# The opening of a streamed encoder layer: TensorE's order held fixed, adaLN weights in other buffers, small loads later, one Newton round, and dt in two passes

## The chip, the cores and the metric

The kernel runs on one core of a Trainium2 chip. It computes in fp32. The metric is the device time of one execution in microseconds; lower is better. One execution of the program was also profiled, and its trace gives the start and length of every instruction on TensorE (PE), VectorE (DVE), ScalarE (ACT), GpSimd (POOL) and the DMA queues that SyncE (SP) and POOL issue.

## The reference

One inference step of a hybrid trunk of two layers, for a prompt of 256 tokens and a sample of 64 (320 together, model width 2048). Each layer modulates an RMS norm by a vector that comes from the condition `c` through a large weight (adaLN), mixes, and adds a gated norm of the result:

```python
def modulate(x, c, w_ada, b_ada, g_pre):
    mod = jax.nn.silu(c) @ w_ada + b_ada
    shift, scale, gate = jnp.split(mod[:, None, :], 3, axis=-1)
    return rms_norm(x, g_pre) * (1 + scale) + shift, gate
...
for layer in range(DEPTH):                      # DEPTH = 2
    hp, gate_p = modulate(xp, c_prompt, ...)    # 256 tokens
    hs, gate_s = modulate(xs, c_sample, ...)    # 64 tokens
    # even layer: one input projection for z, x/B/C, dt, q, k, v, gate;
    # SSD heads and sliding-window attention, one output projection
    # odd layer: u, gb, gc, g; short causal convolution; output projection
    xp = xp + gate_p * rms_norm(op, norm_post[layer])
```

In the even layer `dt = softplus(dt_raw + dt_bias)` has 32 columns, one for each SSD head. The outputs are both token streams and the new caches and states.

## The kernel before

**Products.** A token's features lie on partitions: activations are tiles of [128 features, 320 tokens], 16 k-tiles for the width of 2048. Every large product is made of fp32 numbers that are split into a rounded part and a remainder: weights in `wh` and `wl`, activations in `hh` and `hl`. A k-tile of a unit (128 output features) takes three matmuls with 320 columns: `wh x hh`, `wh x hl` and `wl x hh` (lines 168, 169, 170). `split` makes `wh` on ACT (L148) and from it `wl` on DVE (L149), for eight weight tiles [128, 8 x 128] at a time. `block` loads 16 tiles of weights into a pool of three buffers (`wp`, tag `w`), splits them, and appends a job; jobs are run two blocks later, and between quarters of a job `tick` lets other work in.

**Who sets the order.** The program text gives an order, and a scheduler then places each engine's instructions by its own estimate of when their operands are ready. So on PE, matmuls of one unit can stand among those of another, and an adaLN matmul or a transpose can be moved by some places.

**The opening.** The modulation of the first layer is not known when the program starts, so the first 24 units of the input projection (4 of K, 4 of V, then q and gate for two pairs of heads) go by pieces of K: `PIECES = ((0,1),(1,1),(2,2),(4,4),(8,4),(12,4))`, called stages 0 to 5 here (`j` in the code, and the first digit in the names `ws00` to `ws55`). In each stage all 24 units (`s_0` to `s_23`) take that piece, and `start_unit` adds their PSUM into fp32 tiles: with ACT in stage 0 (L404), with DVE behind it (L415, tiles `acc`, `q`, `g`). Between units stand the adaLN matmuls for the next piece: `ada_first` for tiles 0 and 1 (L362, PSUM `adaf`), and `ada_pe` for quarters of a block (L218, PSUM `adap`). `ada_end` copies the sums from PSUM with ACT (L262, `adar`), transposes them on PE (L264, `adat`) and adds the bias on DVE into `mod` (L268, L273, L275). Block 7 of the adaLN is summed on DVE instead (`ada_side`, L249, `adac`, from tiles `adas`). When the sums of a piece are there, `modulate` makes `mt` on DVE (L340), `hh` on ACT (L341) and `hl` on DVE (L342), in segments of 256 and 64 tokens. In stage 5 the V units are transposed on PE (L419, `vp`) before the attention starts. The first matmul behind the opening goes to a PSUM tile `pq`.

**The norm.** `sumsq` squares x with ACT (L324) and adds with DVE (L351) into two sums; these are merged, summed over partitions on PE (`ss0t`), and `rstd` finds the reciprocal root from the bits of the exponent and three Newton rounds (L302 to L307), spreads it over partitions on PE (`r0b`) and copies it to SBUF (`rsb`, L353).

**Small loads.** Thirteen loads for attention and SSD (cached K and V, sinks, convolution weights and states, dt's bias) are issued by POOL right behind `ada_first(0)`.

**dt.** The unit of dt is a unit like the others: 16 k-tiles x 3 matmuls (`pdt`, with `wdth` and `wdtl`), though only 32 of its 128 output rows are used. `steps` and `time_steps` then transpose it to tokens.

## Time and profile before

| | before |
|---|---|
| runs | 2179.76, 2177.35, 2173.21 us; median 2177.35 |
| profiled execution | span 2172.8 us (the three runs lie 0.4 to 7.0 above it) |
| PE busy | 2130.5 us (98%), 15582 matmuls |
| DVE busy | 1417.7 us (65%) |
| ACT busy | 887.1 us (41%) |
| POOL busy | 152.4 us (7%) |
| DMA | 408.81 MB, mean 188 GB/s |

Busy time is the sum of an engine's instructions with overlaps counted once. A wait row reads: engine, output tile and line of the instruction that waited, the engine, tile and line of what it waited for, and then the microseconds in total, the number of times, and the longest. In a timeline row the first number is the start in us from the beginning of the span and the second the length; `x4` at its end means four instructions of the same kind in a row.

### The profile page before, as it was taken

How to read it: one execution, taken by the hardware profiler on the slowest of the kernel's cores; microseconds unless marked ns; L12 is line 12 of the kernel's file. 1: busy time of each engine (PE TensorE's matmuls, PEld its weight loads, DVE VectorE, ACT ScalarE, POOL GpSimd, SP SyncE). 2: the span in 40 equal slices, each digit the busy share in tenths (PEclk: the TensorE clock that was granted, in tenths of full speed). 3: DMA queues.
4: the chain of work that ended last, by engine and by line, in shares of the span. 5: the costliest groups of instructions: out<-in, count | busy, mean ns of one | idle time of the engine just before them, and what ended most of it. 6: DMA issues, size and time to landing. Idle time of an engine off the chain costs nothing.

```text
span 2172.8 us, 38057 instructions
## 1 busy us (share of the span) xinstructions
PE 2130.5 (98%) x15582; PEld 2054.2 (95%) x15582; DVE 1417.7 (65%) x2351; ACT 887.1 (41%) x1446; POOL 152.4 (7%) x370
## 2 busy tenths in 40 slices
PE   7999999999999999999999999999999999999997
PEld 5899988899999999987999999999999999999996
DVE  5876888888577878996755555556345564444444
ACT  5233454543455565355433333333333333333343
POOL 1000000000123123102000000000000000000001
PEclk9999999999999999999999999999999999999998
DMA  8896545466455555776444444545444544444441
GB/s 314 327 325 209 182 156 180 165 225 226 162 197 175 180 177 195 273 257 244 174 161 176 174 167 169 179 157 198 155 166 164 175 171 144 155 153 141 154 155 68
DMA packets 85758, 408.81 MB, mean 188 GB/s; under 512 B 10544, under 2 KB 11472, under 8 KB 46416
## 3 DMA queue, kind: packets, MB, share of 16 engines
q1 hardware_dynamic: 80496, 392.22, 51.4%
q0 software_dynamic: 5088, 14.16, 2.2%
q8 instruction: 122, 2.00, 0.4%
q14 instruction: 52, 0.43, 0.1%
HBM read 400.35 MB, written 5.99 MB: 187 GB/s over the span
## 4 chain that ended last, share of the span: by engine, by line
PE 94%; DVE 2%; DMA 1%; ACT 1%; issue 1%; POOL 0%; SPq 0%; POOLq 0%; ACTq 0%; DVEq 0%
PE pc L168 13%; PE pc L170 13%; PE pc L169 13%; PE s L168 3%; PE s L170 3%; PE s L169 3%; PE px L168 2%; PE px L170 2%; PE px L169 2%; PE pq L168 2%; PE poe L168 2%; PE pod L168 2%; PE pod L170 2%; PE poe L169 2%; PE pq L170 2%; PE pq L169 2%
## 5 line engine op out<-in xcount | busy, mean ns | idle before, releaser
L249 DVE SCALAR_TENSOR_TENSOR adac<-adas,cs,adac 128x512 f32<-128x512 f32 x420 | 300.8, 744 | 56.1 <-DMA adas<-in_wada 56.1
L926 POOL COPY ncc<-cp 128x2 f32<-128x2 f32 x32 | 6.0, 187 | 932.9 <-DVE cp L924 932.9
L218 PE MATMUL adap<-adaw,cs 128*32 128x128 f32 x1152 | 42.2, 277 | 2.5 <-DMA adaw<-in_wada 2.5
L218 PEld LDWEIGHTS adap<-adaw,cs 128*32 128x32 f32 x1152 | 30.9, 110 | 10.8 <-issue 6.8
L500 ACT ACTIVATE pr<-s,mx 128x192 f32<-128x192 f32 (+2 forms) x80 | 30.0, 388 | 25.2 <-DVE mx L494 16.6
L644 POOL COPY nca<-xp 128x3 f32<-128x3 f32 x24 | 24.2, 1009 | 199.6 <-ACT xp L642 199.6
L931 DVE SCALAR_TENSOR_TENSOR cc<-cp,ccw,cc 128x322 f32<-128x322 f32 x64 | 35.3, 551 | 1.1
L924 DVE TENSOR_TENSOR cp<-pc,u 128x256 f32<-128x256 f32 x31 | 13.2, 425 | 30.6 <-PE pc L170 30.4
L341 ACT ACTIVATE hh<-mt,mod 128x256 fp32r<-128x256 f32 x64 | 23.7, 420 | 20.9 <-DVE mt L340 20.7
L678 ACT ACTIVATE sg<-sg,acum 128x128 f32<-128x128 f32 (+1 forms) x96 | 28.8, 373 | 6.3 <-POOL sg L670 6.3
L415 DVE TENSOR_TENSOR g<-s,g 128x320 f32<-128x320 f32 x40 | 19.0, 485 | 12.3 <-PE s L170 12.3
L649 DVE SCALAR_TENSOR_TENSOR cv<-xp,cw,cv 128x323 f32<-128x323 f32 x48 | 26.4, 551 | 0.3
L939 DVE TENSOR_TENSOR sgg<-pc,sgg 128x320 f32<-128x320 f32 x31 | 15.2, 489 | 17.3 <-PE pc L170 17.1
L849 DVE TENSOR_TENSOR oo<-poe,oo 128x320 f32<-128x320 f32 x16 | 7.9, 492 | 25.6 <-PE poe L170 25.6
L415 DVE TENSOR_TENSOR q<-s,q 128x320 f32<-128x320 f32 x40 | 18.9, 486 | 8.0 <-PE s L170 7.8
L362 PE MATMUL adaf<-w,cs 128*32 128x128 f32 x128 | 10.2, 308 | 13.6 <-ACT ss L324 13.1
L415 DVE TENSOR_TENSOR acc<-s,acc 128x320 f32<-128x320 f32 x32 | 15.3, 488 | 11.3 <-PE s L170 11.2
L342 DVE SCALAR_TENSOR_TENSOR hl<-mt,mod,hh 128x256 fp32r<-128x256 f32 x64 | 21.5, 379 | 1.4 <-ACT hh L341 1.4
L362 PEld LDWEIGHTS adaf<-w,cs 128*32 128x32 f32 x128 | 8.0, 123 | 14.5 <-ACT ss L324 13.0
L531 PE MATMUL o<-pts,vt 128*64 128x256 f32 (+1 forms) x128 | 19.5, 400 | 0.1
L262 ACT ACTIVATE adar_None<-adap 128x128 f32<-128x128 f32 x23 | 6.3, 273 | 32.5 <-PE adap L218 28.4
L491 DVE TENSOR_REDUCE mx<-s 128x2 f32<-128x384 f32 (+2 forms) x40 | 17.1, 469 | 2.7 <-PE s L487 2.5
(2525 smaller groups left out, 8760.5 us busy)
## 6 DMA issues: line engine op xcount, KB each, us to landing
wc<-in_wio SPq DMA_DIRECT2D x124, 1024.0 KB, 4.9
adas<-in_wada SPq DMA_DIRECT2D x224, 256.0 KB, 5.6
adaw<-in_wada SPq DMA_DIRECT2D x36, 1024.0 KB, 6.9
wx<-in_wie SPq DMA_DIRECT2D x24, 1024.0 KB, 5.0
ws<-in_ws SPq DMA_DIRECT2D x21, 1024.0 KB, 6.5
wq<-in_wie SPq DMA_DIRECT2D x16, 1024.0 KB, 4.9
wz<-in_wie SPq DMA_DIRECT2D x16, 1024.0 KB, 4.9
woa<-in_woe SPq DMA_DIRECT2D x16, 1024.0 KB, 4.9
```

What stands on the lines that cost most here:

```text
L168: PE.matmul(ps, lhsT=wh[:, n, :], rhs=xh, start=st, stop=False)
L169: PE.matmul(ps, lhsT=wh[:, n, :], rhs=xl, start=False, stop=False)
L170: PE.matmul(ps, lhsT=wl[:, n, :], rhs=xh, start=False, stop=en)
L218: PE.matmul(ps[32 * q : 32 * q + 32, :], lhsT=cs[:, kt, :], rhs=(w[k] if raw else w[:, k, :])[:, 128 * q : 128 * q + 128], start=kt == 0, ...
L249: V.scalar_tensor_tensor(acc[s], w, c, acc[s], op0=ALU.mult, op1=ALU.add)
L341: S.activation(hi, t[:, a:b], AF.Identity, bias=sh)
L415: V.tensor_tensor(dst, ps, a, op=ALU.add)
L500: S.activation(pr[u // 2][:, u % 2, c0 : c0 + nk], ss[u // 2][:, u % 2, 0:nk], AF.Exp, bias=mx[:, u : u + 1], scale=0.125, accum_out=sm[:, ...
L644: G.tensor_copy(nca[:, ci, 0, :], xp[:, 256:259])
L649: V.scalar_tensor_tensor(cv, xp[:, n : n + 323], cw[:, ci, n : n + 1], cv, op0=ALU.mult, op1=ALU.add)
L678: S.activation(sgs[b][n][:, h, :], sgs[b][n][:, h, :], AF.Exp, bias=acum[0:nt, b, hd : hd + 1])
L931: V.scalar_tensor_tensor(cv, xp[:, m : m + 322], ccw[:, c, m : m + 1], cv, op0=ALU.mult, op1=ALU.add)
```

## The change

1. A small class `PE` stands in for the engine: while `pin[0]` is true, from the first modulation to the end of the opening, each matmul and transpose is told to keep its place in the program's order. At the opening's end all jobs are run (`flush`) before the order is free again.
2. The first reciprocal root comes from ACT's Sqrt table, a reciprocal and one Newton round. The two sums are summed over partitions apart; the first of them becomes `base` while the second still grows. The table is loaded early by a dummy Sqrt behind the fourth square. Tile 0 is modulated straight from the PSUM result.
3. The adaLN weights of the opening are loaded as two halves each into tiles of the activations' pool (tag `G`), ahead by a depth that depends on the stage, instead of into `wp`; from stage 2 on two quarters are taken together.
4. The opening's PSUM comes from two pools by turns (three buffers and four) instead of from the first alone.
5. Weights' remainders of the first block are made in two pieces, and the splits of stage 0's other blocks are issued behind tile 0's modulation.
6. The thirteen small loads move behind the first K output in stage 5.
7. dt: the rounded part goes to columns 0 to 31 of one weight tile and the remainder to columns 32 to 63, so that two matmuls for each k-tile do what three did; the two row groups are added as the transposition to tokens is made by a matmul with `two`, a pair of stacked identities.

Comments are taken out too, so that line numbers differ: products stand at L42, transposes at L47, the splits at L162 and L165, DVE's evictions at L466, `mt`, `hh`, `hl` at L365 to L367.

```diff
+    class PE:
+        @staticmethod
+        def matmul(*a, **k):
+            ins = nc.tensor.matmul(*a, **k)
+            return tc.keep_in_program_order(ins) if pin[0] else ins
...
-    def split(dst_h, dst_l, src):
+    def split(dst_h, dst_l, src, parts=1):
         S.activation(dst_h, src, AF.Copy)
-        V.tensor_tensor(dst_l, src, dst_h.bitcast(F32), op=ALU.subtract)
+        n = src.shape[1] // parts
+        for m in range(0, src.shape[1], n):
+            V.tensor_tensor(dst_l[:, m : m + n], src[:, m : m + n], dst_h[:, m : m + n].bitcast(F32), op=ALU.subtract)
...
-        V.tensor_scalar(v, ps, 1.0 / n, EPS, op0=ALU.mult, op1=ALU.add)
-        V.tensor_scalar(vh, ps, -0.5 / n, -0.5 * EPS, op0=ALU.mult, op1=ALU.add)
+        if base is None:
+            V.tensor_scalar(v, ps, 1.0 / n, EPS, op0=ALU.mult, op1=ALU.add)
+        else:
+            V.scalar_tensor_tensor(v, ps, 1.0 / n, base, op0=ALU.mult, op1=ALU.add)
+        V.tensor_scalar(vh, v, -0.5, None, op0=ALU.mult)
...
+        if k == 3:
+            S.activation(wk.tile([128, 1], F32, tag="rt", name="table"), sums[1][:, 0:1], AF.Sqrt)
+    base = mean(by_token(sums[0], "ss0a", ones[:, 0:1]), D, "r0m")
+    rsp = rstd(by_token(sums[1], "ss0t", ones[:, 0:1]), D, "r0", True, base)
     rsb = stile([128, T], "rsb")
-    S.activation(rsb, rstd(by_token(acc0, "ss0t", ones[:, 0:1]), D, "r0"), AF.Copy)
+    S.activation(rsb, rsp, AF.Copy)
...
+    def ada_fetch(depth):
+        while first and len(fetched) < depth:
+            q = first.pop(0)
+            t = [act.tile([128, 2, 512], F32, tag="G", name=f"adaw{q[1]}_{q[2]}{m}") for m in range(2)]
+            for m in range(2):
+                nc.sync.dma_start(t[m], i["wada"][q[0], q[1], q[2]][:, 2 * m : 2 * m + 2, :])
+            fetched.append((q, [t[k // 2][:, k % 2, :] for k in range(4)]))
+    def ada_next(depth):
+        q, raw = fetched.pop(0)
+        ada_pe(*q, raw=raw)
+        ada_fetch(depth)
...
+            gate = G.dma_start(o["nk"][:, u, 0, :], kT[u][:, 128:256])
+            if u == 0:
+                with tc.issue_after(gate.ins):
+                    load_later()
...
-    modulate(xin, rsb, 0, 0, 1, h0)
+    DEPTH = (1, 2, 4, 3, 2, 0)
+    behind = modulate(xin, rsp, 0, 0, 1, h0)
+    pin[0] = True
...
             while left[0] and (total - left[0]) < total * (n + 1) / 19:
-                ada_pe(*first.pop(0))
-                left[0] -= 1
+                for _ in range(2 if j > 1 else 1):
+                    ada_next(DEPTH[j])
+                    left[0] -= 1
...
-                get = once(f"s{j}_{n}")
+                get = once(f"s{j}_{n}", mmps if n % 5 < 3 else lambda name: sps([128, T], name))
...
-            block(src[g], f"ws{j}{g}", en, h0, act if j < 2 else wp)
+            with ExitStack() as order:
+                if j == 0 and g:
+                    for q in behind:
+                        order.enter_context(tc.issue_after(q.ins))
+                block(src[g], f"ws{j}{g}", en, h0, act if j < 2 else wp, 2 if j == 0 and g == 0 else 1)
+    flush()
+    pin[0] = False
...
-            PE.transpose(pd[0:nt, b, :], dtr[:, t0 : t0 + nt], ident[0:32, 0:32])
+            PE.matmul(pd[0:nt, b, :], lhsT=dtr[:, t0 : t0 + nt], rhs=two, start=True, stop=True)
...
+    def dt_unit(src, h, then):
+        w = wp.tile([128, 16, 128], F32, tag="w", name="wdt")
+        nc.sync.dma_start(w, src)
+        get = once("pdt")
+        for hf in range(2):
+            wh = wp.tile([128, 8, 128], F32R, tag="wh", name=f"wdt{hf}")
+            part = w[:, 8 * hf : 8 * hf + 8, :]
+            S.activation(wh, part, AF.Copy)
+            V.tensor_tensor(wh[:, :, 32:64], part[:, :, 0:32], wh[:, :, 0:32].bitcast(F32), op=ALU.subtract)
...
+                    for m in range(2):
+                        PE.matmul(ps[0:96], lhsT=wh[:, n, 0:96], rhs=h[m][kt // 4][:, kt % 4, :],
+                                  start=kt == 0 and m == 0, stop=kt == 15 and m == 1)
```

On PE in stage 0, before the change (`adaf` is tile 1's adaLN, `w_4` to `w_7` its weights, `adat` the transpose that closes a sum):

```order
L264 MATMUL adat_0_0_253<-ident,adar_0_0_251 128x64
L362 MATMUL adaf_370<-w_4_95,cs 32x128 x8
L362 MATMUL adaf_370<-w_5_96,cs 32x128 x5
L168 MATMUL s_0_319<-hh_0_296,ws00h_305 128x320
L168 MATMUL s_1_324<-hh_0_296,ws00h_305 128x320
L168 MATMUL s_2_329<-hh_0_296,ws00h_305 128x320
L169 MATMUL s_0_319<-hl_0_297,ws00h_305 128x320
```

and after it, from the same transpose and then from the end of s_8:

```order
L47 MATMUL adat_0_0_254<-ident,adar_0_0_252 128x64
L42 MATMUL s_0_308<-hh_0_284,ws00h_293 128x320
L42 MATMUL s_0_308<-hl_0_285,ws00h_293 128x320
...
L42 MATMUL s_8_362<-hh_0_284,ws01l_299 128x320
L42 MATMUL adaf_367<-w_4_95,cs 32x128 x8
L42 MATMUL adaf_367<-w_5_96,cs 32x128 x8
L42 MATMUL adaf_367<-w_6_97,cs 32x128 x8
L42 MATMUL adaf_367<-w_7_98,cs 32x128 x8
L47 MATMUL adat_0_1_402<-ident,adar_0_1_400 128x64
```

The 13 adaLN matmuls ahead of the first product (two records each in the trace, of 26) have moved behind s_8, and adat stands right behind them; every adat of the opening does now.

On DVE where stage 2 ends and stage 3 begins, before the change:

```order
L415 TENSOR_TENSOR g_295<-s_23_1152,g_295 128x320
L149 TENSOR_TENSOR ws30l_1031<-ws_1028,ws30h_1030 128x1024
L149 TENSOR_TENSOR ws30l_1121<-ws_1028,ws30h_1120 128x1024
L273 TENSOR_TENSOR mod_134<-adat_3_None,bada 128x2x4
```

and after it (of the eight rows of hl the first and the last):

```order
L466 TENSOR_TENSOR g_283<-s_23_1181,g_283 128x320
L265 SCALAR_TENSOR_TENSOR adac_7_0_719<-adas_7_5_1015,cs,adac_7_0_719 128x512
L265 SCALAR_TENSOR_TENSOR adac_7_1_720<-adas_7_5_1015,cs,adac_7_1_720 128x512
L367 SCALAR_TENSOR_TENSOR hl_1_1074<-mt_4_1075,mod_134,hh_1_1073 128x256
...
L367 SCALAR_TENSOR_TENSOR hl_1_1074<-mt_7_1096,mod_134,hh_1_1073 128x64
L265 SCALAR_TENSOR_TENSOR adac_7_0_719<-adas_7_6_1169,cs,adac_7_0_719 128x512
L165 TENSOR_TENSOR ws30l_1114<-ws_1111,ws30h_1113 128x1024
```

Eleven instructions, eight of them hl of tiles 4 to 7, stand between the eviction of s_23 and ws30l where there were none. PE's first products of stage 3 are `hh x ws30h`, `hl x ws30h` and `hh x ws30l` of one unit, in this order.

On PE in stage 5, before the change, the transposes of a V unit (s_4 is the first of them):

```order
L170 MATMUL s_5_2414<-hh_3_2178,ws51l_2309 128x320
L168 MATMUL s_5_2414<-hh_3_2178,ws51h_2308 128x320
L419 MATMUL vp_0_2405<-ident,vT_2403 128x128
L419 MATMUL vp_1_2408<-ident,vT_2403 128x128
L419 MATMUL vp_3_2411<-ident,vT_2403 64x128
```

and after it:

```order
L42 MATMUL s_4_2441<-hl_3_2216,ws51h_2345 128x320
L42 MATMUL s_4_2441<-hh_3_2215,ws51l_2346 128x320
L47 MATMUL vp_0_2456<-ident,vT_2454 128x128
L47 MATMUL vp_1_2459<-ident,vT_2454 128x128
L47 MATMUL vp_3_2462<-ident,vT_2454 64x128
```

Seven products of s_5 stood between the end of s_4 and its transposes; now none does.

More of the change, by code (lines that the diff above doesn't have):

```diff
@@ L33, in hybrid_stream_step, with transpose @@
     nc = tc.nc
-    V, S, G, PE = nc.vector, nc.scalar, nc.gpsimd, nc.tensor
+    V, S, G = nc.vector, nc.scalar, nc.gpsimd
+    pin = [False]
+    class PE:
[3 more added lines that the diff above has]
+            return tc.keep_in_program_order(ins) if pin[0] else ins
+        @staticmethod
+        def transpose(*a, **k):
+            ins = nc.tensor.transpose(*a, **k)
+            return tc.keep_in_program_order(ins) if pin[0] else ins
     const = ctx.enter_context(tc.tile_pool(name="const", bufs=1))
@@ L320, in by_token, with mean @@
         return ps
+    def mean(ps, n, name):
+        b = wk.tile([128, 3], F32, tag="rb", name=name)
+        V.tensor_scalar(b, ps, 1.0 / n, EPS, op0=ALU.mult, op1=ALU.add)
+        return b
     def sumsq(acc, t, first, name):
@@ L371, in hybrid_stream_step, with load_later @@
     vt = [stile([128 if n < 3 else 64, 512], f"vt{n}") for n in range(4)]
-    for p in range(4):
-        G.dma_start(kT[p][:, 256:384], i["cachekT"][:, p, :])
-    G.dma_start(vt[2], i["cachev"])
-    sinks = load("sinks", i["sinksT"], ep, G)
-    cw = load("cw", i["convaw"], ep, G)
-    cb = load("cb", i["convab"], ep, G)
-    dskip = load("dskip", i["dskipT"], ep, G)
-    nssm = load("nssm", i["normssm"], ep, G)
-    dtb = load("dtb", i["dtb"], ep, G)
-    cprev = load("cprev", i["cprev"], ep, G)
-    alog = ep.tile([128, NH], F32, name="alog")
-    G.dma_start(alog, i["alog"].to_broadcast([128, NH]))
+    sinks, cw, cb, dskip, nssm, cprev = (ep.tile(list(i[n].shape), F32, name=n) for n in
+                                         ("sinksT", "convaw", "convab", "dskipT", "normssm", "cprev"))
+    dtb = ep.tile([64, 1], F32, name="dtb")
+    alog = ep.tile([128, NH], F32, name="alog")
+    def load_later():
+        for p in range(4):
+            G.dma_start(kT[p][:, 256:384], i["cachekT"][:, p, :])
+        G.dma_start(vt[2], i["cachev"])
+        G.memset(dtb, 0.0)
+        G.dma_start(dtb[0:32], i["dtb"])
+        for t, n in ((sinks, "sinksT"), (cw, "convaw"), (cb, "convab"), (dskip, "dskipT"), (nssm, "normssm"),
+                     (cprev, "cprev")):
+            G.dma_start(t, i[n])
+        G.dma_start(alog, i["alog"].to_broadcast([128, NH]))
     nca = ep.tile([128, 24, 2, 3], F32, name="nca")
@@ L575, in hybrid_stream_step @@
     dec = ep.tile([128, 3, NH], F32, name="dec")
+    two = ep.tile([64, NH], F32, name="two")
+    V.tensor_tensor(two, ident[0:64, 0:32], ident[0:64, 32:64], op=ALU.add)
     def steps(ps):
-        dtr = stile([32, T], "dtr")
-        V.tensor_scalar(dtr, ps[0:32, :], dtb[:, 0:1], None, op0=ALU.add)
+        dtr = stile([64, T], "dtr")
+        V.tensor_scalar(dtr, ps[0:64, :], dtb[:, 0:1], None, op0=ALU.add)
         tasks.append(time_steps(dtr))
@@ L629, in time_steps, with mm @@
             G.dma_start(acs_b[b, :, 0:nt], at[:, t0 : t0 + nt])
-    unit(wie[16], "dt", h0, steps)
+    def dt_unit(src, h, then):
[7 more added lines that the diff above has]
+            V.tensor_tensor(wh[:, :, 32:64], part[:, :, 0:32], wh[:, :, 0:32].bitcast(F32), op=ALU.subtract)
+            def mm(hf=hf, wh=wh):
+                ps = get()
+                for n in range(8):
+                    kt = 8 * hf + n
+                    for m in range(2):
+                        PE.matmul(ps[0:96], lhsT=wh[:, n, 0:96], rhs=h[m][kt // 4][:, kt % 4, :],
+                                  start=kt == 0 and m == 0, stop=kt == 15 and m == 1)
+                    if n % 4 == 3:
+                        yield
+                if hf:
+                    then(ps)
+            jobs.append(mm)
+            while len(jobs) > LOOK:
+                run()
+    dt_unit(wie[16], h0, steps)
     bTs, cTs, xss, zs = {}, {}, {}, {}
```

20 lines of the change are left out of this document (11 added, 9 removed).

## The prediction

> **What bounds the kernel now.** I read the page's head first, then the chain of waits, then busy time by stretches, then PE's waits in the first 300 us.
>
> ```profile
> span 2172.8 us, 38057 instructions
> PE 2130.5 (98%) x15582; PEld 2054.2 (95%) x15582; DVE 1417.7 (65%) x2351; ACT 887.1 (41%) x1446; POOL 152.4 (7%) x370
> PE 94%; DVE 2%; DMA 1%; ACT 1%; issue 1%; POOL 0%; SPq 0%; POOLq 0%; ACTq 0%; DVEq 0%
> ...
> 0.00:25.00 25.00, 10.68 (x104) 8.57 (x105) 13.24 (x46) 10.95 (x24) 10.13 (x24) 1.00 0.93 336
> 25.00:40.00 15.00, 13.88 (x110) 12.38 (x111) 5.67 (x11) 11.56 (x27) 0.00 (x0) 1.00 1.03 417
> 40.00:60.00 20.00, 17.46 (x206) 14.75 (x204) 16.57 (x36) 7.67 (x13) 0.00 (x0) 1.00 0.65 215
> 60.00:98.00 38.00, 36.10 (x419) 31.28 (x418) 30.19 (x61) 8.00 (x14) 0.00 (x0) 0.96 0.87 322
> 98.00:240.00 142.00, 141.85 (x1262) 135.75 (x1263) 104.19 (x184) 48.12 (x72) 5.42 (x10) 1.00 0.73 257
> 1060.00:2145.00 1085.00, 1085.00 (x7444) 1083.38 (x7443) 565.45 (x742) 380.11 (x465) 20.99 (x123) 1.00 0.47 161
> ```
>
> A stretch's columns are its length, then PE, weight loads, DVE, ACT and POOL with their counts, granted clock, DMA share and GB/s. PE is 98% busy and 94% of the chain, and from 98 us on it has next to no holes. So two things can move the time: what PE loses before 98 us, and the number of matmuls. What starts the solid stretch later ends the program later by as much. PE's waits in the stream before 98 us, and one ahead of it, with the time in total, their number and the longest:
>
> ```profile
> PE s L168 <- ACT hh L341: 3.2, 2, 1.8
> PE s L169 <- DVE hl L342: 1.1, 1, 1.1
> PE s L168 <- DVE g L415: 0.8, 1, 0.8
> PE s L170 <- DVE ws30l L149: 0.5, 1, 0.5
> PE adat L264 <- ACT adar L262: 0.5, 1, 0.5
> ...
> 59.50:63.50 4.00, 3.98 (x20) 2.74 (x24) 3.62 (x9) 0.61 (x2) 0.00 (x0) 0.59 0.97 372
> ```
>
> The first four rows lie in the stream of products and sum to 5.6 us. The last row is a stretch right behind such a wait: the granted clock is 0.59, only 20 matmuls run in 4 us, and against full clock 4 x (1 - 0.59) = 1.6 is lost, about 1.9 with the edges of the slow time outside this window. So 7.5 us can be won in the stream. On the other side DVE is 83% busy from 40 to 60 us and 79% from 60 to 98: where PE may not step around a late operand, it pays for it.
>
> **Prices** come from these rows (start, length, what runs; in the bracket the idle time before, and its releaser):
>
> ```profile
> 28.46 0.31 PE L169 MATMUL s<-hl,ws00h 128*128 128x320 f32 x1
> 28.60 0.31 PE L170 MATMUL s<-hh,ws00l 128*128 128x320 f32 x1
> 30.60 2.37 PE L362 MATMUL adaf<-w,cs 128*32 128x128 f32 x38
> 55.20 0.41 PE L168 MATMUL s<-hh,ws12h 128*128 128x320 f32 x1
> 27.28 3.43 ACT L404 ACTIVATE acc<-s 128x320 f32<-128x320 f32 x8 [2.60 <-PE s L170]
> 31.99 1.05 ACT L148 ACTIVATE ws10h<-ws 128x1024 fp32r<-128x1024 f32 x1
> 91.67 0.49 DVE L415 TENSOR_TENSOR g<-s,g 128x320 f32<-128x320 f32 x1 [0.39 <-PE s L170]
> 92.08 2.35 DVE L149 TENSOR_TENSOR ws30l<-ws,ws30h 128x1024 fp32r<-128x1024 f32 x2
> 98.02 1.27 DVE L342 SCALAR_TENSOR_TENSOR hl<-mt,mod,hh 128x256 fp32r<-128x256 f32 x4
> 70.09 1.40 DVE L249 SCALAR_TENSOR_TENSOR adac<-adas,cs,adac 128x512 f32<-128x512 f32 x2
> ```
>
> A product matmul takes 0.146 us (28.46 to 28.60, and three of them 0.44), an adaf record 0.063 (2.37 / 38), an eviction on ACT 0.43 (3.43 / 8), a split 1.05 on ACT and 1.18 on DVE, one adac 0.7, one tile's hl 0.64, an eviction on DVE 0.4 to 0.49.
>
> **The head, -1.6.** Today the reciprocal root starts from bits and takes three rounds:
>
> ```profile
> 13.76 0.49 DVE L351 TENSOR_TENSOR ss<-ss,ss 128x320 f32<-128x320 f32 x1
> 16.57 0.16 DVE L306 TENSOR_TENSOR r0t<-r0t,r0h 128x3 f32<-128x3 f32 x1
> 16.77 0.16 DVE L307 SCALAR_TENSOR_TENSOR r0y<-r0t,r0y 128x3 f32<-128x3 f32 x1
> 2.60 1.28 ACT L100 ACT_TABLE_LOAD   x1 [2.60 <-DMA cT<-in_cT]
> 3.89 0.23 ACT L100 ACTIVATE cs<-cT 128x32 f32<-128x32 f32 x1
> 11.52 1.55 ACT L324 ACTIVATE ss<-x 128x320 f32<-128x320 f32 x4 [0.28 <-DMA x<-in_xT]
> 26.68 0.41 PE L169 MATMUL s<-hl,ws00h 128*128 128x320 f32 x1 [1.11 <-DVE hl L342]
> ```
>
> Eight small DVE operations go and one reciprocal comes: 7 x 0.2 (16.57 to 16.77) = 1.4 less. The merge of the two sums (0.49) leaves the path. [...] That makes -1.05. The Sqrt table is loaded among the first squares, where ACT waits for each part of x (0.28 before the last); uncovered, it would cost 1.0 more. Tile 0's hl stands behind one halved split in place of two, and it was waited for by 1.11 us: another -0.5. Together -1.6, bounds -2.2 and -0.3. [...]
>
> **Stage 0 (K tile 0), +3.4.** Of tile 1's adaLN matmuls, 26 records run today in PE's dead time ahead of the first product; in the fixed order all stand behind s_8: 26 x 0.063 = 1.65. Right behind them stands their transpose, adat, which waits 0.5 for ACT as in the row above. ACT then has adar and tile 1's hh ahead of the evictions from s_8 on: 16 x 0.43 and two splits make 9.0 us, against 15 x 0.44 = 6.6 on PE. I take half of the 2.4 (1.25), since seven PSUM buffers let PE run on. Bounds +2.1 (none of it) and +4.6 (all).
>
> **Stage 1, +0.1.** DVE has 24 evictions, four splits, mod, mt and hl in both kernels; I expect waits to be swapped for others. Bounds -1 and +1.5.
>
> **Stage 2 into 3, +3.6.**
>
> ```profile
> 98.15 0.71 PE L168 MATMUL s<-hh,ws30h 128*128 128x320 f32 x3 [1.46 <-ACT hh L341]
> 59.52 0.56 PE L168 MATMUL s<-hh,ws20h 128*128 128x320 f32 x2 [1.75 <-ACT hh L341]
> ```
>
> Today PE steps ahead in stage 3 while ws30l is made (a wait of 0.5) and later waits 1.46 for hh, 2.1 with the restart. After the change DVE's queue holds, between stage 2's last eviction (g from s_23) and ws30l, two adac (1.4), eight hl rows for four tiles (2.5), another adac (0.7) and the split (1.2): 5.8, and with the eviction 6.2, less the two matmuls that PE may still run and the start of the eviction, about 5.7. 5.7 - 2.1 = +3.6. Bounds -2.1 (DVE is ready) and +4.5. **The clock, 0**: behind the wait of 1.75 it fell; behind the one of 1.46 three products took 0.71, no longer than elsewhere. I count one slow time before and one after, now behind the 5.7; bounds -1.9 (none) and +1.9 (two). [...]
>
> **Stages 3 to 5, +3.7.**
>
> ```profile
> 205.98 0.55 PE L419 MATMUL vp<-ident,vT 128*128 128x128 f32 x3
> 21.87 0.27 ACT L262 ACTIVATE adar<-adaf 64x128 f32<-64x128 f32 x1 [1.65 <-PE adaf L362]
> ```
>
> Twelve quarter blocks of adaLN now run in pairs. A product behind a quarter takes 0.41 in place of 0.31, and I take as much on entry: 6 x 0.2 = -1.2. Four adat stand directly behind their sums: 4 x 0.5 = +2.0; or 4 x 1.57 where ACT is in a split. V's transposes (vp), today without a wait, stand directly behind their unit and wait for its eviction and a crossing: 0.49 + 0.23 (the wait of 0.5 less adar's 0.27) = 0.72, 4 x 0.72 = +2.9; at least 4 x 0.4, at most 4 x 1.5 behind a split. pq, the first matmul behind the opening, today at 240.1 (the end of the fifth stretch above), then starts at 240.1 - 1.6 + 3.4 + 0.1 + 3.6 + 3.7 = 249.3.
>
> **dt, -2.3.**
>
> ```profile
> L168 PE MATMUL pdt<-hh,wdth x16: 309/309/415, 395.8 to 403.3; 128*128 128x320 f32 x16
> kT<-in_cachekT POOLq DMA_DIRECT2D x4, 64.0 KB, 6.2
> vt<-in_cachev POOLq DMA_DIRECT2D x1, 256.0 KB, 6.9
> 76.32 2.14 ACT L148 ACTIVATE ws22h<-ws 128x1024 fp32r<-128x1024 f32 x2 [0.44 <-DMA ws<-in_ws]
> ```
>
> One of three such passes of 16 goes: 16 x 0.146 = -2.3. The low half of its split shrinks on DVE, which is off the path there, and three transposes become three matmuls of the same size.
>
> **Costed at nothing.** The small loads (these two rows are 0.51 of about 0.65 MB, 1.6 us of all queues at the 417 GB/s above) leave the saturated time; since ACT and DVE end stages 0 and 1, this wins 0 to 1.6. At their new place they queue on POOL behind the first K output; attention needs them some 30 us later, and they land within 7; without that cover, 7. SP issues two halves per adaLN quarter, and the deeper prefetch can save the 0.44 for which a split waited for ws. The second PSUM pool frees by the same evictions. The DVE sums for later blocks start two steps later: +0.3, bounds 0 and 1.
>
> **Sum.** -1.6 + 3.4 + 0.1 + 3.6 + 0 + 3.7 - 2.3 + 0.3 = +7.2, so a span of 2180.0. The profiled 2172.8 lies 4.5 below the median of the runs shown (2177.35); the forecast is **2184**, just under 2184.5.
>
> **Rivals.**
>
> *The fixed order gives a smooth stream* (faster, 0.15). If DVE is ready when stage 2 ends, all 7.5 us of waits and slow clock go: -1.6 + 1.65 - 7.5 - 1.2 + 2.0 + 1.6 (vp at 0.4) - 2.3 = -7.3, time 2170. For it: DVE has 3.4 + 7.8 us free between 40 and 98. Against: its rows ahead of ws30l stand behind the last eviction, where earlier free time is no use. It decides from a wait at ws30l under 1 us.
>
> *Old waits for new ones* (same, 0.32). The wait for ws30l comes, but no slow clock, adat costs 0.27 and vp 0.4 each, and ACT doesn't end stage 0: -1.6 + 2.15 + 0.1 + 3.6 - 1.9 - 1.2 + 1.1 + 1.6 - 2.3 + 0.3 = +1.9, time 2179. For it: one clock drop in a trace is thin evidence, and ACT is busy only 34% of 98 to 240.
>
> *Each fixed transpose meets a split* (slower, 0.13). adat 6.3 and vp 6.0, 7.4 more than counted: +14.6, time 2192. For it: DVE is 73% busy from 98 to 240; against it, ACT's 34%.
>
> That the order isn't held gets no chance: the built program shows it held.
>
> **How the numbers follow.** The forecast has 0.40, and 2181 to 2188 as its own range. About 0.3%, 6.5 us, can be told from no change, and 2184 lies at that bound; with the 0.13 I put 0.53 on slower, 0.32 on same, 0.15 on faster. The range, 2169 to 2193, takes in the rivals and leaves out what lies beyond the first and third.
>
> **What would show it.** The first product with hl by 25 us, or the head failed. A wait of PE for ws30l of over 4 us near 100, with a granted clock near 0.5 behind it. Waits at adat and vp of 0.4 to 0.8. pq's first matmul at 248 to 251. pdt in 32 matmuls and 4.7 us. I am wrong above all if stage 3 starts before 98 or the transposes of V cost nothing.

## The result: 0.73% slower, and the profile after

| | before | after |
|---|---|---|
| median of the runs | 2176.45 us (4 runs) | 2192.08 us (4 runs, 2191.43 to 2197.96) |
| ratio to before, 95% interval | | 1.0073 (1.0061 to 1.0085) |
| profiled span | 2172.8 us | 2189.6 us |
| half clock, from the first clock record to the program's tail | 3.4 us | 17.1 us |

Half clock means stretches in which the granted clock of TensorE is 0.50 in the profile. The sign was forecast; of the size, +7.2 us in the span, less than half. The span grew by 16.8 us, the median of the runs by 15.6. The measured 2192 lies outside the forecast's own range, 2181 to 2188, and inside the wide one that took in the rivals. A table of landmarks, the start of the first matmul with certain weights in both traces, shows where:

| landmark | before | after | difference |
|---|---|---|---|
| stage 1 (ws10) | 40.5 | 42.8 | +2.3 |
| stage 2 (ws20) | 59.5 | 62.7 | +3.2 |
| stage 4 (ws40) | 148.1 | 154.3 | +6.2 |
| stage 5 (ws50) | 196.1 | 202.7 | +6.6 |
| pq, the opening is over | 240.1 | 250.0 | +9.9 |
| pz, dt is over (wz00) | 403.7 | 411.0 | +7.3 |
| second SSD group (wx10) | 640.9 | 649.8 | +8.9 |
| last SSD group (wx30) | 807.7 | 816.0 | +8.3 |
| SSD half of the output projection (wot0) | 926.0 | 939.7 | +13.7 |
| odd layer, second channel tile (wc10) | 1048.2 | 1065.0 | +16.8 |

So the opening lost 9.9, dt won 2.6, and 9.5 more went far behind the change, between pz and 1065 us. First the opening. PE's waits in the first 310 us of the changed kernel (total, times, longest), the rows of over 1 us in the stream:

```profile
PE adat_None L47 <- ACT adar_None L278: 3.4, 7, 0.8
PE s L42 <- DVE ws30l L165: 2.9, 1, 2.9
PE vp L47 <- DVE vT L466: 2.8, 4, 0.9
PE s L42 <- DVE hl L367: 2.5, 2, 1.7
PE s L42 <- DVE q L466: 2.0, 1, 2.0
PE s L42 <- ACT hh L366: 1.9, 1, 1.9
PE s L42 <- DVE ws22l L165: 1.4, 1, 1.4
```

These stand against the rows of before with 3.2 (hh), 1.1 (hl), 0.8 (an eviction) and 0.5 (ws30l). The seven waits at adat and the four at vp are new. The place where stage 3 begins, from PE's timeline and then DVE's:

```profile
95.52 0.42 PE L42 MATMUL s<-hh,ws30h 128*128 128x320 f32 x1 [0.38 <-ACT ws30h L162]
97.64 0.63 PE L42 MATMUL s<-hl,ws30h 128*128 128x320 f32 x1 [1.70 <-DVE hl L367]
101.21 0.64 PE L42 MATMUL s<-hh,ws30l 128*128 128x320 f32 x1 [2.94 <-DVE ws30l L165]
```

```profile
95.18 0.49 DVE L466 TENSOR_TENSOR g<-s,g 128x320 f32<-128x320 f32 x1 [0.39 <-PE s L42]
95.59 1.41 DVE L265 SCALAR_TENSOR_TENSOR adac<-adas,cs,adac 128x512 f32<-128x512 f32 x2
96.91 2.45 DVE L367 SCALAR_TENSOR_TENSOR hl<-mt,mod,hh 128x256 fp32r<-128x256 f32 x8
99.28 0.75 DVE L265 SCALAR_TENSOR_TENSOR adac<-adas,cs,adac 128x512 f32<-128x512 f32 x1
99.94 2.36 DVE L165 TENSOR_TENSOR ws30l<-ws,ws30h 128x1024 fp32r<-128x1024 f32 x2
```

The DVE works without a gap, in the order that the built program showed, and PE stands 0.38 + 1.70 + 2.94 = 5.0 us. Far behind, near 880, a new row stands in PE's waits; here with DVE's and ACT's timelines around it:

```profile
882.40 0.66 PE L42 MATMUL adap<-adac,es 128*32 128x128 f32 x8 [2.51 <-DVE adac L265]
```

```profile
880.09 1.23 DVE L165 TENSOR_TENSOR wos2l<-wos,wos2h 128x1024 fp32r<-128x1024 f32 x1 [1.66 <-ACT wos2h L162]
881.23 2.16 DVE L265 SCALAR_TENSOR_TENSOR adac<-adas,cs,adac 128x512 f32<-128x512 f32 x2
```

```profile
878.58 0.53 ACT L852 ACTIVATE ea<-ea 128x384 f32<-128x384 f32 x1 [4.14 <-DMA ea<-acs_t]
879.01 1.04 ACT L162 ACTIVATE wos2h<-wos 128x1024 fp32r<-128x1024 f32 x1
```

ACT waits 4.14 us for a transfer of the SSD part, the split wos2h is queued behind it, on DVE wos2l waits for that split, behind it stand the last two sums of an adaLN block, and PE's sum over partitions waits for those. The kernel before has the same wait of ACT for `ea` (a tile of the SSD part; 3.75 us at 871.40), but no block of the side sums ended just then. Last, stretches of 3.41 us, or two of them, ahead of and at half clock:

```profile
93.81:97.22 3.41, 1.75 (x11) 1.25 (x9) 3.02 (x7) 2.00 (x2) 0.00 (x0) 1.00 1.04 407
97.22:104.05 6.83, 3.47 (x11) 2.92 (x11) 5.74 (x12) 1.06 (x1) 0.00 (x0) 0.50 0.43 172
878.87:882.28 3.41, 1.02 (x7) 0.76 (x6) 2.19 (x3) 1.62 (x4) 2.14 (x2) 1.00 0.37 138
882.29:889.11 6.82, 6.71 (x33) 3.87 (x35) 3.54 (x7) 3.98 (x11) 1.06 (x2) 0.50 0.86 285
1029.06:1032.47 3.41, 1.53 (x29) 1.10 (x17) 2.59 (x13) 0.74 (x3) 0.00 (x0) 1.00 0.88 327
1032.47:1035.88 3.41, 3.35 (x36) 2.53 (x37) 2.70 (x9) 1.59 (x6) 0.00 (x0) 0.50 0.94 317
```

At half clock a product starts every 0.267 us in place of 0.146 (the products from 101.65 to 103.78), so PE starts 0.55 of the products that it would. As an estimate, half of its busy time there is counted as lost, 1.7 + 3.4 + 1.7 = 6.8 us, against 1.7 in the profile of before (one such stretch, 60.22 to 63.63). Near 880 the wait and the clock together make 2.5 + 3.4 = 5.9 of the 16.8.

### The profile page after: what moved, and what is told of

Read it like the earlier page. It is cut to its first block, busy times and chain, and to the rows that moved or that the text cites. A ratio compares the mean times of both kernels' runs of the same rounds, so it can differ in the third digit from the quotient of the medians.

```text
span 2189.6 us, 38062 instructions
## 1 busy us (share of the span) xinstructions
PE 2131.3 (97%) x15575; PEld 2057.1 (94%) x15575; DVE 1415.8 (65%) x2346; ACT 890.4 (41%) x1450; POOL 152.9 (7%) x371
## 4 chain that ended last, share of the span: by engine, by line
PE 92%; DVE 4%; DMA 2%; ACT 1%; issue 1%; POOL 0%; POOLq 0%; SPq 0%; DVEq 0%; ACTq 0%
PE pc L42 40%; PE s L42 8%; PE px L42 7%; PE pq L42 5%; PE poe L42 5%; PE pod L42 5%; PE poa L42 5%; PE pz L42 4%; PE pot L42 3%; PE adap L42 2%; PE pos L42 1%; PE c L42 1%; PE o L42 1%; PE pt L47 1%; DMA ea<-acs_t 1%
## 5 line engine op out<-in xcount | busy, mean ns | idle before, releaser
L42 PE MATMUL adap<-adaw,cs 128*32 128x128 f32 x1152 | 39.0, 279 | 1.2 <-DMA adaw<-in_wada 1.2
L42 PEld LDWEIGHTS adap<-adaw,cs 128*32 128x32 f32 x1152 | 31.3, 111 | 6.8 <-issue 4.3
L466 DVE TENSOR_TENSOR q<-s,q 128x320 f32<-128x320 f32 x40 | 18.8, 486 | 12.9 <-PE s L42 12.9
L742 DVE SCALAR_TENSOR_TENSOR cv<-xp,convaw,cv 128x323 f32<-128x323 f32 x48 | 26.5, 551 | 0.4
L466 DVE TENSOR_TENSOR g<-s,g 128x320 f32<-128x320 f32 x40 | 18.8, 485 | 10.3 <-PE s L42 10.3
L42 PE MATMUL adaf<-w,cs 128*32 128x128 f32 x128 | 10.4, 320 | 11.9 <-ACT ss L349 11.9
L367 DVE SCALAR_TENSOR_TENSOR hl<-mt,mod,hh 128x256 fp32r<-128x256 f32 x64 | 21.2, 379 | 1.2 <-ACT hh L366 1.2
L763 POOL TENSOR_SCALAR_AFFINE_SELECT sg<-sg 128x512 f32<-128x512 f32 (+1 forms) x24 | 17.3, 726 | 42.6 <-DMA sg<-acs_b 42.5
L466 DVE TENSOR_TENSOR acc<-s,acc 128x320 f32<-128x320 f32 x32 | 15.4, 488 | 7.3 <-PE s L42 6.9
L42 PEld LDWEIGHTS adaf<-w,cs 128*32 128x32 f32 x128 | 8.1, 128 | 12.7 <-ACT ss L349 11.9
L42 PE MATMUL o<-pts,vt 128*64 128x256 f32 (+1 forms) x128 | 19.5, 400 | 0.1
```

The costliest lines, as they stand in the source:

```text
L42: ins = nc.tensor.matmul(*a, **k)
L367: il = V.scalar_tensor_tensor(h[1][g][:, k, a:b], t[:, a:b], sh, hi.bitcast(F32), op0=ALU.add, op1=ALU.subtract)
L466: V.tensor_tensor(dst, ps, a, op=ALU.add)
L742: V.scalar_tensor_tensor(cv, xp[:, n : n + 323], cw[:, ci, n : n + 1], cv, op0=ALU.mult, op1=ALU.add)
L763: G.affine_select(sg, sg, pattern=[[0, 4], [1, nt]], base=0, channel_multiplier=-1, compare_op=ALU.is_ge, fill=NEG)
```

## The experiments

For each kernel the table has the span of its profile, what half clock took in that profile (half of PE's busy time in those stretches; the program's tail left out), and the ratio of the runs to those of the kernel before on the same chip.

| kernel | span | lost at half clock | the rest | ratio, 95% interval |
|---|---|---|---|---|
| before | 2172.8 | 1.7 | 2171.1 | 1 |
| after | 2189.6 | 6.8 | 2182.8 | 1.0073 (1.0061 to 1.0085) |
| 1 later sums in their old phase | 2188.6 | 6.4 | 2182.2 | 1.0054 (1.0039 to 1.0069) |
| 2 order left free | 2180.5 | 6.4 | 2174.1 | 1.0027 (1.0017 to 1.0036) |
| 3 before, dt alone | 2175.2 | 3.0 | 2172.3 | 0.9990 (0.9981 to 0.9999) |
| 4 block 7's sums from stage 3 | 2182.0 | 5.1 | 2176.9 | 1.0036 (1.0026 to 1.0046) |
| 5 before, dt and block 7's sums | 2170.2 | 0 | 2170.2 | 0.9997 (0.9987 to 1.0007) |
| 6 fixed order, transposes later | 2190.2 | 14.4 | 2175.9 | 1.0058 (1.0043 to 1.0072) |
| 7 Sqrt table first | 2191.0 | 10.9 | 2180.1 | 1.0060 (1.0045 to 1.0075) |
| 8 small loads back | 2189.9 | 6.5 | 2183.4 | 1.0074 (1.0058 to 1.0090) |
| 9 four repairs, order free | 2171.0 | 1.7 | 2169.3 | 0.9980 (0.9971 to 0.9989) |
| 10 four repairs, order fixed | 2177.6 | 6.3 | 2171.3 | 1.0006 (0.9997 to 1.0015) |
| 11 PE kept busy in one wait | 2191.8 | 9.7 | 2182.1 | 1.0070 (1.0057 to 1.0084) |
| 12 as 9, other phase of the sums | 2178.8 | 6.3 | 2172.5 | 1.0009 (1.0000 to 1.0018) |

What half clock takes differs from run to run of one program (the mean granted clock was 0.994 to 0.996 over the runs of the kernel before, 0.990 to 0.994 over those of kernel 4), so "the rest" compares the profiles better than the span, and the ratio of many runs has the last word.

**1. The later sums in their old phase.** A generator issues the DVE sums of later adaLN blocks step by step; each quarter of a job adds a fraction to what is due, and each whole one due is a step. Here 2.2 steps are due at its start, what the quarters added before the change between its start and the end of the opening's jobs.

```diff
     side["rate"] = RATE_A
+    side["due"] = 2.2
```

> The changed kernel, with the generator of the DVE sums for the later blocks started with 2.2 steps due, so that its steps fall on the same quarters of the stream as before the change; nothing else differs. Theory A (the loss far behind the opening comes from the generator's late start: PE waits 2.5 us for adac near 880 and runs at half clock behind it): pq still starts at about 250, no PE wait for adac over 1 us and no slow clock near 880, and about 5 us less, some 2187. Theory B (that loss belongs to something else that the change moved, such as transfers or buffers): the wait stays or comes elsewhere, and the time stays within 2 us of 2192.

The wait for adac is gone, and so are the slow stretches near 880 and 1030: from wx30 to wot0 it takes 119.4 us, against 123.7 in the changed kernel and 118.3 before. Theory A holds there. It doesn't for the stretch behind, from wot0 to wc10: that takes 125.1 as it did 125.3 (122.2 before), although neither the slow stretch near 1030 nor a wait for wot0l is there. Yet pq came at 253.8, since this run met half clock twice before 70 us, and "the rest" is only 0.6 better: waits for other things grew, for `adaw` from 1.2 to 3.1 and for the odd layer's hh from 1.2 to 2.8. The time was 2191.07, not the 2187 that A named; the ratio fell by 0.0019, some 4 us, with intervals that overlap.

**2. The order left free.**

```diff
-    pin[0] = True
```

> The changed kernel, with the order of TensorE left to the scheduler throughout; all other parts stay. Theory A (the fixed order makes PE wait at each transpose, 3.4 us at adat and 2.8 at vp, and at ws30l): the waits at adat and vp go, the one for ws30l shrinks from 2.9 to under 1.5 as PE may step ahead, and pq starts at 242 to 245 in place of 250. Theory B (DVE's queue and the slower head cost the time, and the order of PE only decides where the waiting shows): pq starts at 248 or later, with as much waiting under other names.

pq started at 241.6, the rest is 8.7 lower. PE's waits up to 242 us:

```profile
PE s L42 <- DVE ws20l L165: 4.4, 1, 4.4
PE s L42 <- ACT ws30h L162: 1.4, 1, 1.4
PE s L42 <- DVE ws22l L165: 0.7, 1, 0.7
PE s L42 <- ACT ws22h L162: 0.6, 1, 0.6
PE s L42 <- DVE hl L367: 0.5, 1, 0.5
```

Nothing waits at vp, 0.4 at adat, and the wait for ws30l is gone, although DVE's queue there is almost unchanged: PE has two adaLN quarters (3.70 us, at 96.89) to do just ahead, and takes products without ws30l first. A new wait of 4.4 at ws20l (at 64.60) shows that DVE is behind as stage 2 begins. The fixed order costs 0.0046 of the 0.0073. Most of what is left doesn't lie in the opening: pq is 1.5 later than before, dt wins that back, and this kernel reaches wx30 at 806.8, 0.9 ahead of the kernel before. From there it loses 5.2 up to wot0 and 3.5 more up to wc10.

**3. dt alone on the kernel before.** The edit is the new `dt_unit`, `steps` and the matmul with `two`, and nothing else of the diff.

> The kernel before, with dt in two passes as the only change. Theory A: 16 matmuls of 0.146 us less, the first product behind dt (pz) starts 2.3 to 2.6 earlier, and all of it reaches the end: 2173.9 where the kernel before has 2176.45. Theory B: a shift of that size moves other work against the stream and a wait further behind takes it back: pz earlier by as much, the end within 1 us of before.

From pq to pz it took 161.2 us in place of 163.6, and the ratio is 0.9990: 2.2 us, which reach the end. In this profile pq came 2.7 later than before, after a wait for hh of 3.4, with nothing changed ahead of it but dt's bias tile and one small DVE instruction for `two`; one profile of the opening is that uncertain.

**4. Block 7's sums from stage 3 on.**

```diff
-        if j == 1:
-            side["gen"], side["rate"] = ada_side([(0, 7)]), RATE_0
+        if j == 3:
+            side["gen"], side["rate"] = ada_side([(0, 7)]), 0.4
```

> The changed kernel, with the DVE sums of block 7 begun in stage 3 at 0.4 steps per quarter in place of stage 1 at 0.24. In the built program the rows of hl now stand ahead of the last eviction of stage 2, and ws30l right behind it. Theory A (the stall at the start of stage 3 is the DVE queue between that eviction and ws30l): PE waits under 2 us there in place of 5.0, without a slow clock, and pq starts at 244 to 246 in place of 250. Theory B (DVE has a fixed amount to do before pq, and PE waits for it sooner or later): stage 3 starts earlier, but waits of the same sum come in stages 3 and 4, and pq starts at 249 or later. The wait for adac near 880 stays by both.

pq at 245.4, as A said, although the waits at stage 3 did not fall as far as written:

```profile
93.69 0.41 PE L42 MATMUL s<-hh,ws30h 128*128 128x320 f32 x1 [0.98 <-ACT ws30h L162]
96.31 0.42 PE L42 MATMUL s<-hh,ws30l 128*128 128x320 f32 x1 [2.07 <-DVE ws30l L165]
```

3.1 in place of 5.0, and half clock behind it all the same. The ratio fell by 0.0037. The sums were not paid again in stages 3 and 4 (stage 4 starts 4.3 earlier than in the changed kernel, pq 4.6), so B falls, and DVE's queue ahead of ws30l made at least 1.9 of the 5.0. The split itself, right behind the last eviction now, is still waited for.

**5. dt and block 7's sums on the kernel before.** The edits of 3 and 4 together, on the kernel before.

> The kernel before, with dt in two passes and the DVE sums of block 7 begun in stage 3 at 0.4 steps per quarter; nothing of the fixed order, the buffers or the head. In the built program ws30l stands ahead of the last eviction of stage 2 there. Theory A (DVE's queue sets PE's waits before stage 3, and it is the adac work that fills it): the waits for hh and ws30l between 55 and 98 us shrink, stage 2 starts 1 to 2 earlier, pq at 236 to 238 in place of 240, and with dt the time is 0.2 to 0.3% under before, 2172 to 2174 where before is 2178. Theory B (the sums only move): pq at 240 or later, and nothing beyond dt's 0.1%.

The profile is what A said: pq at 238.0, no wait for ws30l, no half clock. The runs are not: 0.9997, no better than dt alone. The odd layer's waits for hh are 2.8 there in place of 1.2, which takes back 1.6. What took the rest in the runs stays open. The profiled execution was a lucky one: its time of 2172.11 is the lowest of twelve, which go up to 2182.01.

**6. Transposes one unit later, order fixed.** `ada_end` puts its transpose and what follows on a list, and so does `modulate`; the list is run behind the next unit's eviction. vp likewise:

```diff
+            while pend:
+                pend.pop(0)()
...
-                PE.transpose(pt[0:nt, :], dst[:, t0 : t0 + nt], ident)
+        if vps:
+            v_tokens(*vps.pop(0))
```

> The changed kernel, order still fixed, but each adat and each group of vp stands one unit later in the program, so that its operand has a unit's time to get ready; modulate follows adat. Theory A (the waits at the fixed transposes are paid in full): the 2.8 at vp and most of the 3.4 at adat go, pq starts at 244 to 246 in place of 250, the ratio to before falls from 1.0073 to about 1.005. Theory B (they are hidden in what PE would wait for anyway): pq at 248 or later. The DVE queue ahead of ws30l is as before in both, and so is the wait there, about 5.

The waits at vp fell from 2.8 to 0.6 and those at adat in the stream are gone; the rest is 6.9 lower. pq came at 251.7, which by its number is B's side; less what half clock took ahead of it, it is 251.7 - 9.2 = 242.5, against 250.0 - 1.7 = 248.3. So the waits were paid in full, and the clock took much of the gain back. Of the 6.9, the runs show 0.0015, 3 us, with intervals that overlap. That is no matter of this profile alone, which lost 14.4 at half clock: the mean granted clock of the four runs is 0.989 to 0.991, where the changed kernel has 0.991 to 0.992, an estimated 4 us more. Why this program meets half clock more often stays open.

**7. The Sqrt table ahead of the squares.**

```diff
+    S.activation(wk.tile([128, 1], F32, tag="rt", name="table"), ones[:, 0:1], AF.Sqrt)
     for k in range(KT):
...
-        if k == 3:
-            S.activation(wk.tile([128, 1], F32, tag="rt", name="table"), sums[1][:, 0:1], AF.Sqrt)
```

> The changed kernel, with the Sqrt table loaded ahead of the first square, while ACT still waits for x, in place of behind the fourth. Theory A (the load behind the fourth square holds up the squares, and with them DVE's sums by 1.4 us): DVE has no idle of 1.38 near 8 to 9.8 us, r0v comes 0.5 to 1.4 earlier than 17.33, and the first product with hl starts at 26.1 to 26.9 in place of 27.44. Theory B (DVE's own pace and the two column sums on PE set the head): r0v within 0.3 of 17.33. By either, the time changes by under 2 us.

r0v, the first step behind the column sums, in the changed kernel and then here:

```profile
9.75 4.51 DVE L353 TENSOR_TENSOR ss<-ss,ss 128x320 f32<-128x320 f32 x11 [1.38 <-ACT ss L349]
17.33 0.16 DVE L316 SCALAR_TENSOR_TENSOR r0v<-ss0t,r0m 128x3 f32<-128x3 f32 x1 [1.78 <-PE ss0t L42]
27.44 0.42 PE L42 MATMUL s<-hl,ws00h 128*128 128x320 f32 x1 [0.79 <-DVE hl L367]
```

```profile
15.47 0.16 DVE L316 SCALAR_TENSOR_TENSOR r0v<-ss0t,r0m 128x3 f32<-128x3 f32 x1 [1.12 <-PE ss0t L42]
15.36 4.05 PE L42 MATMUL adaf<-w,cs 128*32 128x128 f32 x34
19.34 1.54 PE L42 MATMUL r0b<-r0d,ones 128*128 128x128 f32 x6
26.34 0.41 PE L42 MATMUL s<-hl,ws00h 128*128 128x320 f32 x1 [0.80 <-DVE hl L367]
```

A holds, with more than was written: r0v 1.9 earlier, the first lo-product 1.1. The other 0.8 goes to PE, where 34 adaLN records now stand ahead of r0b and take 0.12 each. The early load itself is of no use: the load for `cs` at 2.74 follows it, and a third load, of the Sqrt table again, comes at 12.31, behind the squares. There ACT has nothing else to do until r0v ends, so what won is that no load stands among the squares any more.

**8. The small loads back.** `load_later()` is called at the place where the loads stood.

> The changed kernel, with the thirteen small loads back at their old place near 10 us; all else stays. Theory A (ACT, DVE and the fixed order set stages 0 to 2, not transfers): stage starts and pq within 0.5 us, time within 1 us of the changed kernel. Theory B (transfers are what the opening waits for, and the 0.65 MB cost it up to 1.6 us): stages 1 to 3 start 0.8 to 1.6 later, and so does the end.

Stages 1 and 2 start 0.7 later than in the changed kernel and stage 3 1.3; pq less half clock is 249.1 against 248.3, and the ratio is 1.0074 against 1.0073. By the numbers that lies between the two theories. But the first square of x starts 0.66 later in this profile (6.19 in place of 5.53), and the first of the cached K and V is issued only at 9.74: nearly all of the 0.7 was there before the small loads could cost anything. So moving them won nothing up to stage 2, and nothing that the runs can tell.

**9 and 10. Four repairs.** Edits 1, 4 and 7, with the order free as in 2 (kernel 9) or with it fixed and the transposes later as in 6 (kernel 10).

> The changed kernel with four repairs: the order of TensorE left free, the Sqrt table loaded ahead of the squares, the sums of block 7 begun in stage 3, the later sums started with 2.2 steps due. Theory A (the parts add up; taken without the time lost at half clock, the single runs gave -8.7, -2.7, -5.9 and -0.6 against a span of 2182.8, and the first and third overlap): a span without that loss of 2166 to 2169, and a measured time 0.1 to 0.35% under the kernel before. Theory B (each repair moves the wait to the next place): no better than before, ratio 1.000 to 1.002.

> The changed kernel with the order of TensorE still fixed, but each adat and vp one unit later, the Sqrt table ahead of the squares, the sums of block 7 begun in stage 3 and the later sums started with 2.2 steps due. Theory A (a fixed order is no loss by itself where its operands are early enough; the single runs gave -6.9, -2.7, -5.9 and -0.6): a span without half-clock loss of 2167 to 2170, ratio 0.998 to 1.001. Theory B (under a fixed order PE's waits for hh and hl at the head and for PSUM in stage 1 stay, and each brings half clock): ratio 1.001 to 1.004, with three or more slow stretches before 110 us.

Kernel 9 beats the kernel before and the changed one: 2173.78 against 2177.89 before, ratio 0.9980, 0.2% less, pq at 237.6. The parts nearly added up (the rest is 2169.3, where 2166 to 2169 was expected). Under the fixed order the same repairs end at 1.0006: no longer a loss that can be told, but 0.0026 behind the free order. Its longest waits before pq, of which the first (for PSUM, in stage 1) and the third (in the head) are those that B named:

```profile
PE s L42 <- DVE q L484: 2.4, 1, 2.4
PE s L42 <- ACT ws30h L162: 2.3, 1, 2.3
PE s L42 <- ACT hh L375: 1.9, 1, 1.9
PE s L42 <- DVE ws30l L165: 0.9, 1, 0.9
```

and three slow stretches came before 110 us. A's ratio was seen, though not its span (the rest is 2171.3, where 2167 to 2170 was expected), and B's mechanism.

**11. PE kept busy in one wait.**

```diff
+                if j == 3 and n == 0:
+                    get = filled(get)      # 30 matmuls hh x hh into the same PSUM, ahead of its first product
```

> The changed kernel, with 30 matmuls of no use (their sums are overwritten) put ahead of stage 3's first product, where PE waits 5.0 us for hl and ws30l; they take 30 x 0.146 = 4.4. Theory A (the wait itself can't be shortened this way, but the slow clock behind it comes from PE's idleness): stage 3's first product with ws30l starts at the same distance from the end of stage 2, 6.2 to 6.6 us, the granted clock there is 1.00 in the stretch from the end of stage 2 to 10 us behind it, and pq comes 1 to 3 earlier than in the changed kernel at the same start of stage 2. Theory B (the clock falls with the load, or by chance, not with idleness): a slow stretch there all the same, and pq as late or later.

```profile
100.72 4.56 PE L42 MATMUL s<-hh 128*128 128x320 f32 x30
106.95 0.41 PE L42 MATMUL s<-hh,ws30l 128*128 128x320 f32 x1 [1.38 <-DVE ws30l L165]
```

```profile
100.62:104.03 3.41, 3.41 (x25) 3.41 (x24) 3.11 (x8) 2.14 (x3) 0.00 (x0) 1.00 0.99 368
104.04:107.45 3.41, 2.03 (x14) 1.77 (x13) 3.41 (x7) 0.00 (x0) 0.00 (x0) 1.00 0.53 209
```

The product with ws30l comes 6.2 us behind the end of stage 2, as without the filling, and the clock stays at 1.00, where the changed kernel and the kernels 1, 4, 6, 7, 8 and 10 all have half clock. From stage 2's start to pq, less what half clock took on the way (2.7 here, 1.7 in the changed kernel), it took 185.8 and 185.6. So the filling kept the clock and shortened nothing else. In this run half clock came at other places, pq was not earlier (254.4), and the ratio didn't move. That the clock behind the wait hangs on PE's idleness rests on this one profile and on the count in the last section.

**12. The same as 9 with another phase of the later sums.**

```diff
-    side["due"] = 2.2
+    side["due"] = 1.1
```

> The last kernel with four repairs, with 1.1 in place of 2.2 steps due at the start of the later sums. Theory A (what comes far behind the opening hangs on which quarter of the stream a step of the sums falls, and each phase has waits of its own): the span from wx30 (the first product of the last SSD group's first unit) to wc10 (the second tile of the odd layer) changes by 1 to 5 us against 242.8 in the kernel with 2.2 and 249.0 in the changed kernel; the opening stays. Theory B (the lateness alone counts, a step less is harmless): within 1 us of 242.8, and the same time, 2174.

Up to wx30 the kernels are alike (pq 237.4 and 237.6, wx30 802.6 and 803.6). From wx30 to wc10 it takes 251.6 us in place of 242.8, and the ratio is 1.0009 in place of 0.9980: 6 us, for one step's difference. The row that does it, on PE and ACT:

```profile
869.60 0.47 PE L47 MATMUL adat_None<-ident,adar_None 128*128 128x128 f32 x1 [4.61 <-ACT adar_None L278]
...
866.56 0.52 ACT L851 ACTIVATE ea<-ea 128x384 f32<-128x384 f32 x1 [5.65 <-DMA ea<-acs_t]
```

ACT waits 5.65 for `ea`, and adar is queued behind it (with a split and three tiles of the SSD part, it starts at 869.29): the same hole of ACT as in the changed kernel, met by another step of the sums. Theory A, at nearly twice its upper number.

## Why the prediction was right in sign and less than half the size

**The opening was sized right, by terms that were partly wrong.** pq was put at 249.3 and came at 250.0. From stage 2 on the terms held: +7.3 was forecast, +6.7 came. The two that rested on the order of the built program were the best: the wait at stage 3's start was 5.0 (5.7 forecast; 2.9 of it at ws30l itself, where over 4 was named as the sign), with the slow clock behind it and one such loss before and one after; the four adat of stages 3 to 5 cost 2.2 (2.0 forecast) and vp 2.8 (2.9). Three more waits at adat in stages 1 and 2, 1.3 together, and one of 1.4 for ws22l were in no term. Ahead of stage 2, +1.9 was forecast and +3.2 came, out of larger errors of both signs: the head 2.65 too low, stage 0 2.15 too high, stage 1 0.8 too low. That pq came out within 0.7 is in part luck.

**The head failed**: "-1.6" was +1.05. The first lo-product came at 27.44 in place of 26.68, and ahead of it stands one hi-product now, where three stood: 0.3 more is still to do. The new root did better than its term. -1.05 is made of -1.4 for the small operations, -0.49 for the merge and +0.8 for the Sqrt on ACT (they add to -1.1), and the +0.8 counts two crossings between engines at 0.28 each, which no run shows: here r0v ends on DVE at 17.49, the Sqrt runs on ACT from 17.52 to 17.72 and the reciprocal starts on DVE at 17.76, crossings of 0.03 and 0.04. From r0v to r0d it takes 1.23 in place of 2.43, where 0.6 less was forecast. The step that failed is the one that saw the table load covered by ACT's waits for x. The load stands at 7.86, 1.28 long, without a wait ahead of it, and the next square starts only at 9.26: the load held up the squares, DVE stood 1.38, and the merge that was saved was lost again. The second column sum on PE (1.44) was not counted at all. So r0v came 1.55 later, and r0d 0.35. The rest came on PE, before the change and then after it:

```profile
18.55 1.20 PE L312 MATMUL r0b<-r0d,ones 128*128 128x128 f32 x6
19.68 2.15 PE L362 MATMUL adaf<-w,cs 128*32 128x128 f32 x34
```

```profile
19.07 1.54 PE L42 MATMUL r0b<-r0d,ones 128*128 128x128 f32 x6
20.55 3.13 PE L42 MATMUL adaf<-w,cs 128*32 128x128 f32 x38
```

The same work takes longer (four adaLN records more are the smaller part of it), since PE's adaLN records last 421 ns up to 19.26 before and 22.13 after, where the first clock record stands, and 273 behind it (the last section); no term had that. In the three profiles with the old head the first clock record comes at 18.6 to 19.6 and the first lo-product at 26.2 to 26.9, in the six with the new head under the fixed order and the load among the squares at 22.1 to 23.5 and 27.4 to 28.2. Why it comes later with the new head was not tested. Run 7 gave 1.1 of the head back.

**Stage 0 was sized too high**: +3.4 for a measured +1.25. The adaf records took 1.3 more in the stream (64 in 3.69 us in place of 38 in 2.37) and adat 0.4; the 1.25 for ACT's evictions did not come. Stage 1 cost 0.9 in place of 0.1: PE waited 2.0 there for an eviction on DVE.

**dt held**: -2.6 and, alone, -2.2 in the runs, for -2.3.

**What failed by most is a term of 0.3.** The sums for the later blocks were priced at two steps of lateness, with bounds of 0 and 1. Lateness was not what they cost. They moved to another phase against a stream in which ACT waits for `ea` in the last SSD group (3.75 us before, 4.14 in the changed kernel, 5.65 in run 12), and a sum over partitions fell into that hole: 2.5 us of PE's waiting, and 3.4 more at half clock. Run 1 shows that this wait and this slow stretch go with the phase alone; run 12 shows a wait of 4.6 come back with it. Of the 9.5 us lost behind dt, 5.4 lie between wx30 and wot0, 3.1 from there to wc10 (in this profile 1.4 for wot0l and 1.7 at half clock, but run 1 takes as long there without either), and 2.1 in the first SSD group, where a wait of 1.0 for sg is new and one block's sum over partitions (0.65, and its transpose) now falls; 1.1 is won between these. For the last two stretches the cause stays open.

**The clock was a term of 0 with bounds of 1.9** and counted in the opening alone. Over the whole profile half clock took 5.1 more than before, and the profile did not catch a bad execution: the mean granted clock was 0.991 to 0.992 in all four runs of the changed kernel, and 0.994 to 0.996 in the 23 runs of the kernel before that stand beside experiments 1 to 4.

Among the rivals, "old waits for new ones" and "each fixed transpose meets a split" were not seen: vp cost 0.6 to 0.9, adat 0.4 to 0.8. The second of them named 2192, the time that came, by a cause that did not. That half the loss lay outside the opening was in none of them. The other buffers, the second PSUM pool and the halved splits (items 3 to 5 of the change) were not tried apart.

## What to carry to other kernels

When an engine's order is held, read in the built program what the other engines have queued ahead of each operand it will now wait for: those waits could be sized here to within a microsecond from the profile of before. A background generator that steps with the stream has a phase; an edit that starts it a step sooner or later is a change of its own, to be tested by itself, since here one step was worth 6 us, more than twice the whole of dt. Where the bounding engine has a clock to lose, count its waits twice: the time that it stands, and the slow stretch that can follow (near 880, 2.5 us and an estimated 3.4). Where several changes meet, ask at which landmark the time is lost: with the order free the changed program was no later than the kernel before up to wx30, and the rest of its loss had nothing to do with the order.
